# Weight sums of the paired tiles moved from VectorE to accumulating DMAs, and the first stage's splits in another order

## The chip, the cores and the metric

The kernel runs on one core of one Trainium2 chip. The metric is the device time of one execution on that core, in microseconds (us); a result is the median of several runs.

## What is computed

One layer of a streaming encoder trunk, for a prompt of 1024 rows and a sample of 32 rows that share the weights. One combined input projection feeds two branches: a conformer convolution module (GLU, causal depthwise convolution of width 31, layer norm, swish, a SiLU gate) and a Mamba-2 mixer (short convolution, SSD scan in chunks, gated RMS norm). Their outputs are gated, merged, projected, and added to the input and to a gated per-layer embedding.

```python
proj = x @ w_in + b_in                     # x: 1056 x 1024, all branch inputs and gates
u = a_val * sigmoid(a_glu)
u = causal_dwconv(u, ...)                  # width 31: the "taps"
u = silu(layer_norm(u)) * silu(a_gate)
xs, B, C = silu(causal_dwconv(xbc, ...))   # width 4
dt = softplus(dt_raw + dt_bias)
y, h = ssd_scan(xs, dt, A, B, C, h0)
out_b = gated_rmsnorm(y, z) @ w_b_out
merged = sigmoid(g_a) * (u @ w_a_out) + sigmoid(g_b) * out_b
out = layer_norm(alpha * x + merged @ w_out + sigmoid(g_p) * (p @ w_ple))
```

The part that the change touches is the first 48 weight tiles of `x @ w_in` (128 output columns each), the product `p @ w_ple`, and the softplus of `dt` that is worked out beside them.

## The kernel before

Everything is held transposed: 1056 columns (1024 + 32 rows of x, NT in the code) by 128 partitions. An fp32 product is made of three matmuls in the form fp32r (`three`): each operand is split into a rounded part "h" and the rest "l", and w_h x_l, w_l x_h and w_h x_h are summed in PSUM. ScalarE rounds (`act`, line 186), VectorE subtracts (`tt`, line 172: "l" = raw - "h"), so every split is one instruction on each of the two. `load` (line 189) issues from SyncE, in the order of the code, loads as well as stores; an issue waits there until its destination buffer is free and its source is ready, and what is behind it waits too. Matmuls are line 192 (`mm`). `stt` is line 176, `tsc` 181 and 183.

*The first stage* (lines 416 to 796) splits the columns of x (`x_split` for the blocks B11, B12, B21, B22 and the difference D1; `t_split` for the sums N2, T3, T4, which `x_sum` forms in place in the raw tiles `xraw`), makes the embedding product `p @ w_ple` and the dt product. `ple_group(m, g)` is one of 8 x 3 groups of six matmuls; ScalarE evicts each to a tile `pl`, and after the third of an m the tile is stored to the DRAM scratch `d_ple`. The tiles `pl` of m = 0 to 3 are units of a pool U (7 units, handed out in a ring and given back at the store), those of m = 4 to 7 lie in the buffers t3h and t3l. The weights of `p @ w_ple` are four tiles, wq0 to wq3, loaded by `wq_load` and split by `wq_split`. Between groups, `step(n)` takes the next n entries from a list `work` (splits, sums). After the first 12 groups come wq2 and wq3's splits, the 48 matmuls of the dt product (`dt_products`), N2's split, the split of the first pair weight, `dt1`, and then the last 12 groups.

*The pair slots*, s = 1 to 24, one for a pair i = s - 1 of weight tiles. A pair's weights are four 128 x 512 blocks r11, r12, r21, r22 (256 KB each), and the two output tiles are formed from seven products in place of eight, with weights

| product | 0 | 1 | 2 | 3 | 4 | 5 | 6 |
|---|---|---|---|---|---|---|---|
| weight | r11 | r21 + r22 | r11 + r21 + r22 | r12 | r11 + r21 | r12 + r11 + r21 + r22 | r22 |

and X-side operands B11, B12, N2, B21, T3, B22, T4. Each product is 24 matmuls. The tile "sx" carries weights 1, 2 and 5 in turn, and r21 is turned into weight 4 in place. In the profile the split weights are w_0h, w_0l to w_6h, w_6l, and the raw blocks are called r. After product j, `pair_slot` evicts what is finished (ScalarE writes a bank of PSUM out, VectorE adds or subtracts later ones), runs the stages of other work that are due (`run`), and then `prep_act(i, j)` and `prep_dve(i, j)`: a written-out order of the rounding, the subtractions, the sums and the loads by which pair i + 1 is made ready and pair i + 2 loaded. A sum must have its parts loaded, and a part can be loaded anew only when its last reader is done.

*What else runs in these slots.* `todo` holds stages (ld0, ld, st, d0, a0, d1 after product 0; a1 after 2; pm, a2 after 4; d2 after 5; pe, end) into which other work puts its steps: the gates (`ga`, `gb`, stored to `d_gate` by SyncE), `cbS` (ScalarE, from a gate tile, slot 6), the base tiles (`bt`, loaded from x and `d_ple`, stored to `d_base`), the GLU (`uin`, `sg`), the short convolution (`vin`, `cb`), and dt2 to dt10 in slots 1 to 5. dt2 (slot 1, after product 0) is the softplus on VectorE; dt3 (slot 1, after product 2) has two memsets on GpSimd, lines 647 and 648; dt4 (slot 1, after product 5) scans with what they wrote, line 658. Last, `run_fill(limit)` pulls the taps of the width-31 convolution (`cae`, `cao`) from a list until a running estimate of VectorE's time in the slot, `dve[0]`, reaches the limit. What the estimate leaves free is filled with taps as long as the list has any.

After slot 24 a slot is one weight tile, 8 k x 3 groups of 352 columns (`slot`; slots 25 to 67), and then the output projections follow.

Of the kernel before, what the change touches and what calls it, by code (L numbers as in the profile page):

```python
# [129 lines left out]
def emit(nc, tc, I, O, ctx):  # L130
# [57 lines left out]
    def load(dst, src):  # L188
        nc.sync.dma_start(dst, src)
# [305 lines left out]

    def pw_sum(i, dst, a, b):
        if i < len(PAIRS):
            if (i, dst) not in pr:
                pr[i, dst] = raw_tile(dst, f"{dst}_{i}")
            tt(pr[i, dst], pr[i, a], pr[i, b], ALU.add)  # L500
# [264 lines left out]
    for q in range(2):
        t_split("n2", (1, 1), q)
    pw_hi(0, 0, "r11")
    pw_lo(0, 0, "r11")
    dt1()
    pw_sum(0, "sx", "r21", "r22")  # L770
    pw_sum(0, "r21", "r11", "r21")
    pw_load(1, "r11")
    work.extend(xs4("D1") + [(pw_hi, 0, 1, "sx"), (pw_lo, 0, 1, "sx"), (pw_sum, 0, "sx", "r21", "r22"), (pw_hi, 0, 2, "sx"),
                             (pw_lo, 0, 2, "sx")] + xs2("T4"))
# [14 lines left out]
    pw_sum(0, "sx", "r12", "sx")
    pw_load(1, "r12")  # L790
    pw_hi(0, 4, "r21")
    pw_lo(0, 4, "r21")
# [993 lines left out]
```

## Time and profile before

| | |
|---|---|
| median of the runs | 1592.32 us (1592.23 to 1593.13, 3 runs) |
| the profiled execution | 1592.68 us, of which 1591.0 us are the span from its first to its last instruction |
| granted TensorE clock, mean | 0.984 |
| instructions | 26642 |
| the chain that ended last | PE 76%, DVE 12%, DMA 5%, ACT 4% |
| DMA | 208.43 MB, queues busy 41.9% of 16 engines' span; HBM read 156.49 MB, written 50.19 MB |

PE is TensorE, DVE VectorE, ACT ScalarE, POOL GpSimd, SP SyncE, and SPq SyncE's DMA queue. A row of a timeline is the start in us, the duration, the engine, the line, the operation, out<-in with tile names, shape and type, and in brackets how long the engine had idled before and what ended that. A row of waits is who waits, for what, then the total in us, the number of waits and the longest. Times count from the first instruction.

### The profile page before, as it was taken

The page shows a single profiled execution, that of the slowest core. Times are in us where ns is not written, and L with a number is a line of the kernel's source. Part 1 is how long each engine was busy: PE and PEld are TensorE (multiplying, and loading weights), DVE is VectorE, ACT ScalarE, POOL GpSimd, SP SyncE. Part 2 cuts the span into 40 slices and gives each one's busy share as a digit, 9 for nine tenths or more (in the row PEclk, how much of TensorE's full clock was granted, in tenths as well). Part 3 has the DMA queues.
Part 4 walks back from the last instruction along what each step waited for, and adds up shares of the span by engine and source line. Part 5 has one row for each costly group of instructions (what it writes and reads, how often), then busy time and mean ns, then how long its engine had stood idle before and what let it go on. Part 6 is the DMA issues. An engine that isn't in the chain of part 4 may idle for free.

```text
span 1591.0 us, 26642 instructions
## 1 busy us (share of the span) xinstructions
PE 1527.2 (96%) x10823; PEld 1481.8 (93%) x10823; DVE 1296.9 (82%) x1763; ACT 808.6 (51%) x1391; POOL 3.0 (0%) x14
## 2 busy tenths in 40 slices
PE   7899999999999989999999999999798999999997
PEld 6899999999999989999999999999688999999997
DVE  6888899999898599988988889888666887676654
ACT  6654334433434556666675666576564543333333
POOL 0000000000000000000000000000000000000000
PEclk9999999999999999999999999999899999999998
DMA  7252444442231134424252542336636171587422
GB/s 254 108 203 98 155 136 137 136 157 103 87 116 55 55 101 89 112 69 123 77 120 66 110 106 63 88 106 187 187 136 240 61 249 57 199 331 257 144 87 78
DMA packets 134377, 208.43 MB, mean 131 GB/s; under 512 B 28071, under 2 KB 84391, under 8 KB 134254
## 3 DMA queue, kind: packets, MB, share of 16 engines
q1 hardware_dynamic: 134254, 206.72, 41.9%
q8 instruction: 85, 1.39, 0.4%
q14 instruction: 38, 0.31, 0.1%
HBM read 156.49 MB, written 50.19 MB: 130 GB/s over the span
## 4 chain that ended last, share of the span: by engine, by line
PE 76%; DVE 12%; DMA 5%; ACT 4%; issue 2%; SPq 0%; DVEq 0%; ACTq 0%
PE ps L192 75%; DMA d_base<-cb_t 1%; PE ps L992 1%; DVE cao_u L176 1%; DVE cae_u L176 1%; DMA d_yn<-cbo_t 1%; DMA L_t<-d_accp 1%; DMA cat_t<-d_ca 1%; DVE sx L172 1%; DVE cb_t L176 0%; DVE wlo L172 0%; DMA d_gate<-ga_t 0%; DVE dt_u L176 0%; DVE acc_t L172 0%; DVE cb_u L176 0%
## 5 line engine op out<-in xcount | busy, mean ns | idle before, releaser
L176 DVE SCALAR_TENSOR_TENSOR cae_u<-uin_u,par,cae_u 128x1086 f32<-128x1086 f32 x120 | 161.3, 1344 | 0.0
L176 DVE SCALAR_TENSOR_TENSOR cao_u<-uin_u,par,cao_u 128x1086 f32<-128x1086 f32 x112 | 150.5, 1344 | 0.0
L186 ACT ACTIVATE whi<-wraw 128x1024 fp32r<-128x1024 f32 x65 | 68.5, 1054 | 67.5 <-PE ps L192 42.8
L186 ACT ACT_TABLE_LOAD x77 | 98.8, 1283 | 7.1 <-DMA out_conv_b<-vin_t 4.9
L172 DVE TENSOR_TENSOR wlo<-wraw,whi 128x1024 fp32r<-128x1024 f32 x65 | 79.3, 1219 | 24.6 <-ACT whi L186 24.5
L186 ACT ACTIVATE vin_t<-ps,par 128x352 f32<-128x352 f32 (+5 forms) x88 | 39.1, 476 | 107.3 <-PE ps L192 107.3
L186 ACT ACTIVATE L_t<-L_t,tk 128x128 f32<-128x128 f32 (+1 forms) x272 | 80.4, 381 | 0.0
L176 DVE SCALAR_TENSOR_TENSOR cb_t<-vin_t,par,cb_t 128x1059 f32<-128x1059 f32 x60 | 79.1, 1319 | 1.2
L186 ACT ACTIVATE zt_t<-ps,par 128x352 f32<-128x352 f32 x48 | 26.4, 554 | 75.3 <-PE ps L192 75.0
L172 DVE TENSOR_TENSOR acc_t<-acc_t,ps 128x352 f32<-128x352 f32 x72 | 36.6, 518 | 33.1 <-PE ps L192 33.0
L186 ACT ACTIVATE gb_t<-ps,par 128x528 f32<-128x528 f32 x26 | 18.2, 701 | 88.7 <-PE ps L192 74.8
L172 DVE TENSOR_TENSOR M<-ps,E 128x512 f32<-128x512 f32 (+1 forms) x32 | 20.4, 637 | 49.0 <-PE ps L192 45.3
L192 PE MATMUL ps<-n2l,w_2h 128*128 128x264 f32 x192 | 55.5, 289 | 3.7 <-ACT ga_t L186 3.7
L192 PE MATMUL ps<-t3l,w_4h 128*128 128x264 f32 x192 | 54.6, 284 | 2.3 <-ACT ga_t L186 2.3
L192 PE MATMUL ps<-n2h,w_2l 128*128 128x264 f32 x192 | 55.2, 288 | 0.0
L192 PE MATMUL ps<-n2h,w_2h 128*128 128x264 f32 x192 | 55.1, 287 | 0.0
L192 PE MATMUL ps<-t4l,w_6h 128*128 128x264 f32 x192 | 54.6, 285 | 0.3 <-ACT gb_t L186 0.3
L192 PE MATMUL ps<-t3h,w_4l 128*128 128x264 f32 x192 | 54.5, 284 | 0.0
L192 PE MATMUL ps<-t4h,w_6h 128*128 128x264 f32 x192 | 54.4, 284 | 0.0
L192 PE MATMUL ps<-t4h,w_6l 128*128 128x264 f32 x192 | 54.4, 283 | 0.0
L192 PE MATMUL ps<-t3h,w_4h 128*128 128x264 f32 x192 | 54.3, 283 | 0.0
L192 PE MATMUL ps<-x0l_t,whi 128*128 128x352 f32 x117 | 41.9, 358 | 8.9 <-ACT sg_t L186 5.0
(878 smaller groups left out, 5910.4 us busy)
## 6 DMA issues: line engine op xcount, KB each, us to landing
r<-in_w SPq DMA_DIRECT2D x96, 256.0 KB, 3.1
wraw<-in_w SPq DMA_DIRECT2D x39, 512.0 KB, 4.3
L_t<-d_accp SPq DMA_DIRECT2D x30, 512.0 KB, 6.5
d_yn<-cbo_t SPq DMA_DIRECT2D x16, 528.0 KB, 3.6
wraw<-in_wb SPq DMA_DIRECT2D x16, 512.0 KB, 3.6
yraw_t<-d_yn SPq DMA_DIRECT2D x15, 528.0 KB, 7.7
gs_t<-d_gate SPq DMA_DIRECT2D x15, 528.0 KB, 5.9
E<-d_expa SPq DMA_DIRECT2D x56, 128.0 KB, 4.7
```

Source lines behind the costliest of these rows:

```text
L172: nc.vector.tensor_tensor(out, a, b, op)
L176: nc.vector.scalar_tensor_tensor(out, a, s, b, op0, op1)
L186: nc.scalar.activation(out, a, f, **kw)
L192: nc.tensor.matmul(out, l, r, start=start, stop=stop, skip_group_check=more)
L992: nc.tensor.transpose(pX[:nt, j * P:(j + 1) * P], XS[j][:, sl], ident)
```

## The change

The sums of a pair's weights are no longer made by VectorE. Each summed weight gets a tile of its own, s1 (weight 1), s2 (weights 2 and then 5) and s3 (weight 4). SyncE loads the first part into it, and the further parts are added by DMAs that GpSimd issues with `accum_op=ALU.add`: s1 = 21 + 22, s2 = 11 + 21 + 22, to which `pw_s4` adds 12 after weight 2 has been split, and s3 = 21 + 11. So a pair has six loads from SyncE in place of four, and five accumulating DMAs from GpSimd, all of 256 KB; the four additions on VectorE go. r21 is no longer held by itself, and the buffers are r11, r12, r22, s1, s3 with one each and s2 with two. `prep_act` and `prep_dve` have another order: the loads of r11 and s2 for pair i + 2 and of r22 for pair i + 1 stand after product 1, s1 after 3, r12 after 5, s3 after 6, and weight 5 is rounded after product 0 of the following slot.

In the first stage, the splits of wq2 and wq3 come ahead of the sums T3 and N2, N2's and the first weight's splits come from the list `work`, `dt1` comes after D1's four splits in the list that runs beside the last 12 groups, and the tiles `pl` lie elsewhere: those of m = 0 and 1 in n2l, 2 and 3 in t3l, 4 and 5 in t3h, 7 in t3l, and only that of m = 6 is a unit of U. The raw weights of dt, w0, lie in the pair stage's buffer o0h in place of t3l.

```diff
-    RTAG = {"r11": 1, "r12": 1, "r21": 2, "r22": 2, "sx": 1}
+    RTAG = {"r11": 1, "r12": 1, "r22": 1, "s1": 1, "s2": 2, "s3": 1}
...
-    w0 = xpool.tile([P, 8, H], F32, tag="t3l", name="w0", bufs=1)
+    w0 = ppw.tile([P, 8, H], F32, tag="o0h", name="w0", bufs=1)
...
+    PARTS = {"r11": ("11",), "r12": ("12",), "r22": ("22",), "s1": ("21", "22"), "s3": ("21", "11"), "s2": ("11", "21", "22")}
...
     def pw_load(i, n):
         if i < len(PAIRS):
-            t = raw_tile(n, f"{n}_{i}")
-            load(t, I["w1"][2 * i + (n[1] == "2"), :, 512 * (n[2] == "2"):512 * (n[2] == "2") + 512])
-            pr[i, n] = t
+            t = pr[i, n] = raw_tile(n, f"{n}_{i}")
+            load(t, pw_src(i, PARTS[n][0]))
+            for q in PARTS[n][1:]:
+                nc.gpsimd.dma_start(t, pw_src(i, q), accum_op=ALU.add)
+
+    def pw_s4(i):
+
+        if i < len(PAIRS):
+            nc.gpsimd.dma_start(pr[i, "s2"], pw_src(i, "12"), accum_op=ALU.add)
...
     def prep_act(i, pos):
         if pos == 0:
+            pw_hi(i, 5, "s2")
             pw_hi(i, 6, "r22")
-        for j, n in {0: ((0, "r11"),), 2: ((1, "sx"),), 4: ((2, "sx"), (3, "r12")), 5: ((4, "r21"),), 6: ((5, "sx"),)}.get(pos, ()):
+        for j, n in {0: ((0, "r11"),), 2: ((1, "s1"),), 3: ((2, "s2"),), 4: ((3, "r12"),), 5: ((4, "s3"),)}.get(pos, ()):
             pw_hi(i + 1, j, n)
 
     def prep_dve(i, pos):
         if pos == 0:
-            pw_lo(i, 5, "sx")
-            pw_sum(i + 1, "sx", "r21", "r22")
+            pw_lo(i, 5, "s2")
         elif pos == 1:
             pw_lo(i, 6, "r22")
             pw_lo(i + 1, 0, "r11")
-            pw_sum(i + 1, "r21", "r11", "r21")
             pw_load(i + 2, "r11")
+            pw_load(i + 1, "r22")
+            pw_load(i + 2, "s2")
         elif pos == 3:
-            pw_lo(i + 1, 1, "sx")
-            pw_sum(i + 1, "sx", "r21", "r22")
+            pw_lo(i + 1, 1, "s1")
+            pw_load(i + 2, "s1")
+        elif pos == 4:
+            pw_lo(i + 1, 2, "s2")
+            pw_s4(i + 1)
         elif pos == 5:
-            pw_lo(i + 1, 2, "sx")
             pw_lo(i + 1, 3, "r12")
-            pw_sum(i + 1, "sx", "r12", "sx")
             pw_load(i + 2, "r12")
         elif pos == 6:
-            pw_lo(i + 1, 4, "r21")
-        if pos == 2:
-            pw_load(i + 2, "r21")
-            pw_load(i + 2, "r22")
+            pw_lo(i + 1, 4, "s3")
+            pw_load(i + 2, "s3")
...
-        if g == 0 and m in (4, 6):
-            both = xpool.tile([P, 2, NT], F32, tag=f"t3{'hl'[m // 2 - 2]}", name=f"pl{m}", bufs=1)
+        if g == 0 and m in (0, 2, 4, 7):
+            both = xpool.tile([P, 2, NT], F32, tag={0: "n2l", 2: "t3l", 4: "t3h", 7: "t3l"}[m], name=f"pl{m}", bufs=1)
...
-    work.extend(xs4("B11") + xs4("B12") + xs2("D1") + [(wdt_split,)] + xs4("B21") + xs4("B22") + xs2("T3") + xs2("N2"))
+    work.extend(xs4("B11") + xs4("B12") + xs2("D1") + [(wdt_split,)] + xs4("B21") + xs4("B22") + [(wq_split, 2), (wq_split, 3)])
...
-    for i in (2, 3):
-        wq_split(i)
+    pw_load(0, "r22")
+    work.extend(xs2("T3") + xs2("N2") + ts2("n2", (1, 1)) + [(pw_hi, 0, 0, "r11"), (pw_lo, 0, 0, "r11")])
+    step(len(work))
     for k in range(8):
         dt_products(k)
...
-    dt1()
...
+    work.extend(xs4("D1") + [(dt1,), (pw_load, 1, "r11"), (pw_hi, 0, 1, "s1"), (pw_lo, 0, 1, "s1"), (pw_load, 1, "s1"), (pw_hi, 0, 2, "s2"),
+                             (pw_lo, 0, 2, "s2"), (pw_s4, 0), (pw_load, 1, "s2")] + xs2("T4"))
```

On ScalarE in the first stage, the rows around the tenth eviction of `pl` (it fills the tile of m = 3 from bank ps13) stand before as follows; wq2h and wq3h are the rounding of the third and fourth w_ple tile, n2h that of N2, x7h the last of the splits of x.

```order
L186 ACTIVATE x6h_t13_116<-xraw_u4_152 128x528
L186 ACTIVATE pl_u8_309<-ps13_302 128x352
L186 ACTIVATE x7h_t15_118<-xraw_u4_152 128x528
L186 ACTIVATE pl_u8_309<-ps14_314 128x352
L186 ACTIVATE pl_u8_309<-ps15_324 128x352
L186 ACTIVATE wq2h_334<-wq2_155 128x512
L186 ACTIVATE wq3h_338<-wq3_157 128x512
L186 ACTIVATE n2h_3_4_390<-xraw_u3_150 128x1056
L186 ACTIVATE n2h_3_4_390<-xraw_u4_152 128x1056
L186 ACTIVATE w0_0h_396<-r11_0_162 128x512
L186 ACT_TABLE_LOAD
```

And now the same stretch, where pl2 is the tile of m = 2 and 3 in t3l, and pl4 that of m = 4 and 5.

```order
L186 ACTIVATE x6h_t13_116<-xraw_u4_152 128x528
L186 ACTIVATE pl2_276<-ps13_307 128x352
L186 ACTIVATE x7h_t15_118<-xraw_u4_152 128x528
L186 ACTIVATE wq2h_317<-wq2_155 128x512
L186 ACTIVATE pl2_276<-ps14_321 128x352
L186 ACTIVATE wq3h_329<-wq3_157 128x512
L186 ACTIVATE pl2_276<-ps15_333 128x352
L186 ACTIVATE n2h_3_4_348<-xraw_u3_150 128x1056
L186 ACTIVATE n2h_3_4_348<-xraw_u4_152 128x1056
L186 ACTIVATE w0_0h_354<-r11_0_162 128x512
L186 ACTIVATE pl4_413<-ps16_406 128x352
```

The unit u8 of the ring U no longer takes the eviction, the two w_ple splits have moved ahead of the last two evictions, and behind w0_0h comes the first eviction of the last 12 groups, where the table load of `dt1` stood.

On GpSimd, from the memset of the dt weights (the last instruction of its set-up) on, before:

```order
L212 MEMSET mask_76 128x128
L213 AFFINE_SELECT mask_76<-mask_76 128x128
L465 MEMSET wdt_143 128x8x64
L647 MEMSET dt3_u12_403 32x1056
L648 MEMSET dt3_u12_403 32x17
```

And now, where the number behind s1, s2, s3 is the pair, line 489 is the accumulating DMA of `pw_load`, 494 that of `pw_s4`, and 651 and 652 are the memsets of dt3:

```order
L464 MEMSET wdt_143 128x8x64
L489 DMA s1_0_164<-in_w1 128x512
L489 DMA s2_0_167<-in_w1 128x512 x2
L489 DMA s3_0_173<-in_w1 128x512
L489 DMA s1_1_518<-in_w1 128x512
L494 DMA s2_0_167<-in_w1 128x512
L489 DMA s2_1_552<-in_w1 128x512 x2
L489 DMA s3_1_574<-in_w1 128x512
L489 DMA s2_2_672<-in_w1 128x512 x2
L651 MEMSET dt3_u8_459 32x1056
L652 MEMSET dt3_u8_459 32x17
L489 DMA s1_2_743<-in_w1 128x512
```

The memsets that the scan of dt4 reads now stand on GpSimd behind the two accumulating DMAs into s2 of pair 2.

On SyncE in slot 6 (before with pair 6's r12, then two loads of x for the base tiles and two stores of gates):

```order
L189 DMA r12_6_1804<-in_w1 128x512
L189 DMA bt_u21_1865<-in_xT 128x1056
L189 DMA bt_u22_1867<-in_xT 128x1056
L189 DMA d_gate_94<-ga_t37_1596 128x1056
L189 DMA d_gate_94<-gb_t38_1597 128x1056
```

And now:

```order
L189 DMA r12_6_1833<-in_w1 128x512
L189 DMA s3_6_1863<-in_w1 128x512
L189 DMA bt_u18_1895<-in_xT 128x1056
L189 DMA bt_u19_1897<-in_xT 128x1056
L189 DMA d_gate_94<-ga_t37_1620 128x1056
L189 DMA d_gate_94<-gb_t38_1621 128x1056
```

The load of s3 stands between r12 and the four transfers of the base and gate tiles.

More of the change, by code (lines that the diff above doesn't have):

```diff
@@ L417, in emit @@
     wq = []
-    QTAG = ("r12", "sx", "r21", "r21")
-    RTAG = {"r11": 1, "r12": 1, "r21": 2, "r22": 2, "sx": 1}
+    RTAG = {"r11": 1, "r12": 1, "r22": 1, "s1": 1, "s2": 2, "s3": 1}
     def raw_tile(tag, name):
@@ L427, in wq_load @@
     def wq_load(i):
-        wq.append([raw_tile(("r12", "sx", "r21", "r22")[i], f"wq{i}")])
+        wq.append([raw_tile(("r12", "s1", "r22", "s2")[i], f"wq{i}")])
         load(wq[i][0], I["wp"][i])
@@ L478, in emit, with pw_src @@
     pr, pw = {}, {}
+    PARTS = {"r11": ("11",), "r12": ("12",), "r22": ("22",), "s1": ("21", "22"), "s3": ("21", "11"), "s2": ("11", "21", "22")}
+    def pw_src(i, q):
+        return I["w1"][2 * i + (q[0] == "2"), :, 512 * (q[1] == "2"):512 * (q[1] == "2") + 512]
     def pw_load(i, n):
         if i < len(PAIRS):
-            t = raw_tile(n, f"{n}_{i}")
-            load(t, I["w1"][2 * i + (n[1] == "2"), :, 512 * (n[2] == "2"):512 * (n[2] == "2") + 512])
-            pr[i, n] = t
+            t = pr[i, n] = raw_tile(n, f"{n}_{i}")
[5 more added lines that the diff above has]
+            nc.gpsimd.dma_start(pr[i, "s2"], pw_src(i, "12"), accum_op=ALU.add)
     def pw_hi(i, j, n):
@@ L494, in pw_lo @@
             tt(l_, pr[i, n], h_[:, :].bitcast(F32), ALU.subtract)
[L496 to L500, printed above, removed]
     def prep_act(i, pos):
         if pos == 0:
+            pw_hi(i, 5, "s2")
             pw_hi(i, 6, "r22")
-        for j, n in {0: ((0, "r11"),), 2: ((1, "sx"),), 4: ((2, "sx"), (3, "r12")), 5: ((4, "r21"),), 6: ((5, "sx"),)}.get(pos, ()):
+        for j, n in {0: ((0, "r11"),), 2: ((1, "s1"),), 3: ((2, "s2"),), 4: ((3, "r12"),), 5: ((4, "s3"),)}.get(pos, ()):
             pw_hi(i + 1, j, n)
@@ L575, in ple_group @@
             three(ps[:, :GN], wh[:, w], wl[:, w], ph[:, k, c0:c1], pl_[:, k, c0:c1], k == 0, k == 1)
-        if g == 0 and m in (4, 6):
-            both = xpool.tile([P, 2, NT], F32, tag=f"t3{'hl'[m // 2 - 2]}", name=f"pl{m}", bufs=1)
+        if g == 0 and m in (0, 2, 4, 7):
+            both = xpool.tile([P, 2, NT], F32, tag={0: "n2l", 2: "t3l", 4: "t3h", 7: "t3l"}[m], name=f"pl{m}", bufs=1)
             pls[m], pls[m + 1] = both[:, 0, :], both[:, 1, :]
-        if g == 0 and m < 4:
+        if g == 0 and m == 6:
             pls[m] = U.get([P, NT], F32, "pl")
@@ L583, in ple_group @@
             load(d_ple[m], pls[m])
-            if m < 4:
+            if m == 6:
                 U.put(pls[m])
@@ L743, in step @@
             f(*a)
-    for n in ("r11", "r21", "r22", "r12"):
+    for n in ("r11", "s1", "s2", "r12", "s3"):
         pw_load(0, n)
@@ L753, in emit @@
     xs2 = lambda n: [(x_sum, n, q) for q in range(2)]
-    work.extend(xs4("B11") + xs4("B12") + xs2("D1") + [(wdt_split,)] + xs4("B21") + xs4("B22") + xs2("T3") + xs2("N2"))
+    ts2 = lambda n, q: [(t_split, n, q, i) for i in range(2)]
+    work.extend(xs4("B11") + xs4("B12") + xs2("D1") + [(wdt_split,)] + xs4("B21") + xs4("B22") + [(wq_split, 2), (wq_split, 3)])
     for m in range(4):
@@ L760, in emit @@
     step(len(work))
-    for i in (2, 3):
-        wq_split(i)
+    pw_load(0, "r22")
+    work.extend(xs2("T3") + xs2("N2") + ts2("n2", (1, 1)) + [(pw_hi, 0, 0, "r11"), (pw_lo, 0, 0, "r11")])
+    step(len(work))
     for k in range(8):
         dt_products(k)
[L765 to L768, printed above, removed]
-    dt1()
[L770 to L774, printed above, removed]
+    work.extend(xs4("D1") + [(dt1,), (pw_load, 1, "r11"), (pw_hi, 0, 1, "s1"), (pw_lo, 0, 1, "s1"), (pw_load, 1, "s1"), (pw_hi, 0, 2, "s2"),
+                             (pw_lo, 0, 2, "s2"), (pw_s4, 0), (pw_load, 1, "s2")] + xs2("T4"))
     for m in range(4, 8):
@@ L781, in emit @@
     x_put((1, 1))
-    for n in ("r21", "r22"):
-        pw_load(1, n)
     pw_hi(0, 3, "r12")
     pw_lo(0, 3, "r12")
+    pw_load(1, "r12")
     for q in range(2):
@@ L788, in emit @@
     x_put((0, 1))
[L789 to L792, printed above, removed]
+    pw_hi(0, 4, "s3")
+    pw_lo(0, 4, "s3")
+    pw_load(1, "s3")
     for q in range(2):
@@ L795, in emit @@
     x_put((1, 0))
-    pw_hi(0, 5, "sx")
     new_psum("ps1")
@@ L1465, in half_load @@
     def half_load(q):
-        pr["h", q] = raw_tile(("r11", "r21")[q], f"half{q}")
+        pr["h", q] = raw_tile(("r11", "s1")[q], f"half{q}")
         load(pr["h", q], I["w_src"][S_CL][:, 512 * q:512 * q + 512])
```

## Prediction

> **What bounds the kernel now.** First the page's busy times and windows by stage, then TensorE's waits stage by stage, then the engines' timelines where it waits. From the page and one table of windows (columns: window, length, then busy time and count of PE, PEld, DVE, ACT, POOL; granted clock, DMA share, GB/s):
>
> ```profile
> PE 1527.2 (96%) x10823; PEld 1481.8 (93%) x10823; DVE 1296.9 (82%) x1763; ACT 808.6 (51%) x1391; POOL 3.0 (0%) x14
> ...
> 20.00:40.00 20.00, 14.24 (x73) 13.43 (x72) 14.96 (x25) 9.93 (x19) 0.00 (x0) 0.83 0.48 184
> 60.00:80.00 20.00, 18.67 (x140) 18.24 (x138) 18.91 (x31) 9.05 (x17) 1.09 (x2) 0.92 0.15 53
> 160.00:200.00 40.00, 37.33 (x305) 36.91 (x305) 34.93 (x43) 14.89 (x23) 0.00 (x0) 1.00 0.49 161
> 200.00:520.00 320.00, 320.00 (x2636) 320.00 (x2635) 291.30 (x368) 128.28 (x216) 0.00 (x0) 1.00 0.34 114
> ```
>
> TensorE is the bound: 1527 of 1591 us. From 200 to 520 us, most of the pair slots, it never pauses, although VectorE is 91% busy beside it. There a matmul takes 320/2636 = 0.121 us, a product of 24 takes 2.91 us, a slot of seven 20.4 us. Work taken off VectorE in that stretch buys nothing by itself; the change can only win where TensorE waits. Its waits, from three windows (0 to 80, 80 to 200, 500 to 620) and one late (1060 to 1240; columns: total us, times, longest):
>
> ```profile
> PE ps L192 <- DVE wq2l L172: 4.4, 1, 4.4
> PE ps L192 <- ACT ga_t L186: 3.7, 1, 3.7
> ...
> PE ps L192 <- DVE ga_t L172: 2.3, 3, 1.5
> PE ps L192 <- ACT ga_t L186: 2.3, 1, 2.3
> PE ps L192 <- DVE sg_t L172: 1.3, 1, 1.3
> ...
> PE ps L192 <- ACT sg_t L186: 5.0, 1, 5.0
> PE ps L192 <- DVE vin_t L172: 3.5, 1, 3.5
> ...
> PE ps L192 <- ACT acc_t L186: 6.9, 4, 4.4
> PE ps L192 <- DVE M L172: 6.9, 1, 6.9
> ```
>
> The late ones lie beyond slot 57; by the order, the list of conv taps is as long in both kernels from slot 49 on, so I leave them at zero. What can move is about 8 us in the prologue, 6 us in slots 2 to 7, 8.5 us around slots 24 and 25.
>
> **The change, part by part.** The sums that go (columns: count, total us, mean ns, idle before), and the two loads between which an accumulating DMA must lie (size, us to landing):
>
> ```profile
> L172 DVE TENSOR_TENSOR sx<-r,r 128x512 f32<-128x512 f32 x48 | 33.2, 692 | 1.7
> L172 DVE TENSOR_TENSOR r<-r,r 128x512 f32<-128x512 f32 x24 | 16.4, 684 | 0.0
> L172 DVE TENSOR_TENSOR sx<-r,sx 128x512 f32<-128x512 f32 x24 | 16.4, 684 | 0.0
> ...
> r<-in_w SPq DMA_DIRECT2D x66, 256.0 KB, 3.1
> wraw<-in_w SPq DMA_DIRECT2D x39, 512.0 KB, 4.3
> ```
>
> VectorE loses 33.2 + 16.4 + 16.4 = 66 us, 2.7 us a slot. Where conv taps are in stock, the order fills the space with them at once; only in slots without taps (1 to 4, 8, 9, 13, 17, 18) does it get ahead.
>
> No accumulating DMA is in this trace. It fetches 256 KB and also reads 256 KB at its destination, so I bound it by 3.1 us (a plain load of its size) and 7.5 us (between the 7.0 of the wait for a d_gate store and the 8.0 of a d_ple store, below), and take 3.7, the middle of the two rows above. GpSimd's own share of an issue is unseen too: 0 to 1.1 us, I take 0.7, above an SP issue. The Trainium skill ("DMA: Bandwidth & Descriptors", section "Anatomy of one DMA — SWDGE (gpsimd) path") gives about 2.0 us and the bytes over 436 GB/s, by which I estimate 2.6 us here; plain loads of that size took 3.1, above that rule, so the rows stand.
>
> *Prologue.* ScalarE, its issuer's stores, VectorE, GpSimd and two TensorE starts:
>
> ```profile
> 27.75 0.46 ACT L186 ACTIVATE pl_u<-ps 128x352 f32<-128x352 f32 x1 [5.97 <-PE ps L192]
> 28.11 0.63 ACT L186 ACTIVATE x7h_t<-xraw_u 128x528 fp32r<-128x528 f32 x1
> ...
> 33.02 2.25 ACT L186 ACTIVATE n2h<-xraw_u 128x1056 fp32r<-128x1056 f32 x2 [2.53 <-DVE xraw_u L176]
> ...
> 48.59 1.51 ACT L186 ACTIVATE pl<-ps 128x352 f32<-128x352 f32 x4
> ...
> 20.50 9.29 SPq L189 DMA_DIRECT2D d_ple<-pl_u  x4
> ...
> d_ple<-pl_u SPq DMA_DIRECT2D x4, 528.0 KB, 8.0
> ...
> 54.74 1.26 DVE L172 TENSOR_TENSOR t3l<-xraw_t,t3h 128x1056 fp32r<-128x1056 f32 x1 [2.40 <-DMA d_ple<-pl]
> ...
> 60.63 0.29 DVE L183 TENSOR_SCALAR dt_u<-dt_u 128x264 f32<-128x264 f32 x1
> ...
> 68.61 0.69 DVE L172 TENSOR_TENSOR w_5l<-sx,w_5h 128x512 fp32r<-128x512 f32 x1
> ...
> 77.49 2.35 DVE L658 TENSOR_TENSOR_SCAN dtc_t<-dt_u,dt_u 32x1056 f32<-32x1056 f32 x1
> 79.77 0.67 DVE L172 TENSOR_TENSOR ga_t<-ga_t,ps 128x528 f32<-128x528 f32 x1
> ...
> 68.80 0.97 POOL L647 MEMSET dt_u<- 32x1056 f32 x1 [66.14 <-DVE dt_u L176]
> ...
> 59.08 0.39 PE L192 MATMUL ps<-n2l,w_2h 128*128 128x264 f32 x1 [3.69 <-ACT ga_t L186]
> ...
> 80.49 0.39 PE L192 MATMUL ps<-x0l_t,w_1h 128*128 128x264 f32 x1 [1.49 <-DVE ga_t L172]
> ```
>
> The tenth `pl` eviction takes a U unit still being stored: 20.5 + 8.0 is about the 27.75 at which it ran, although the view names PE. In the new code `pl` lies in other buffers, so x7h follows at about 22, and the `w_ple` splits stand ahead of the T3 and N2 sums: the 4.4 us wait goes, n2h starts near 29.1 in place of 33.0 (the splits and four sums now fill VectorE from 22.8), and the last `pl` eviction ends near 44.7 in place of 50.1, 5.4 us earlier. t3l waits for the store behind it, so it, dt2 and w_5l come 5.3 us earlier: dt2 at 55.3, w_5l at 63.3. ScalarE no longer has w_5h ahead of the ga_t eviction, so product 2 of slot 1 starts near 51.4 in place of 59.08.
>
> Then two waits are next. Product 5 would start at 51.4 + 3 x 2.91 = 60.1 but needs w_5l, which stands behind dt2: 63.9. And GpSimd's memset for the scan, done 7 us early today, now stands behind the accumulates for pair 2, whose buffer w_5l frees: w_5l, w_6l, w_0l to 65.1; two SP issues ahead of the load 0.9 (the two bt loads below took 0.91); load 3.1, landing at 69.1; first accumulate 3.7, second's issue 0.7, memsets 1.1: 74.6; scan 2.35, ga_t 0.6: slot 2's product 1 starts at 77.6. Queued behind the scan are that ga_t, w_4l and slot 2's dt work; TensorE alone is hurt, being ready at 63.9 + 8.7 = 72.6. Against 80.49 it gains 2.9. But the 3.69 us wait at 59.08 left the clock at 0.92 of 20 us, some 1.6 us lost, while the 2.3 us wait for ACT ga_t, which lies in the window from 160 to 200, left that window at 1.00; a 3 to 5 us pause here will cost about half that: 0.8. Net gain **2.1**, from 4 (everything lands in 3.1) to a loss of 3 (7.5). The Trainium skill ("TensorE: Matmul & The Clock Gate", "Part 1: The HAM clock gate") has the clock halve after an idle window of about 3.4 us; the 2.3 and 3.69 waits agree, and by it the pause at slot 2 would cost the full 1.6.
>
> *Slots 2 to 4.* The waits at the starts of slots 3 and 4 (0.4 of the 2.3 for DVE ga_t, 1.3 for sg_t) come from VectorE running late in slots without taps; 2.7 us less a slot hides both: gain **1.7**. What is late next there is the fourth accumulate for w_5h, with the whole slot as cover.
>
> *Slot 6.* Here ScalarE waits for a store, and TensorE (2.3) for ScalarE:
>
> ```profile
> 164.85 0.91 SPq L189 DMA_DIRECT2D bt_u<-in_xT  x2
> 165.85 0.38 SPq L189 DMA_DIRECT2D d_gate<-ga_t  x1
> ...
> 164.94 0.69 DVE L172 TENSOR_TENSOR w_4l<-r,w_4h 128x512 fp32r<-128x512 f32 x1
> ...
> 173.21 1.08 ACT L186 ACTIVATE cbS_t<-ga_t 128x1056 f32<-128x1056 f32 x1 [7.02 <-DMA d_gate<-ga_t]
> ```
>
> SP's last load of a slot, s3, now waits for w_4l (done near 165.6) and stands ahead of bt and d_gate: 1.25 us later. Beside their 2.1 MB come one load and one accumulate, 0.5 to 0.75 MB at 7 us for 2.1: 1.7 to 2.5 us if all lies on the path. I take **2.5 lost** in all, bounds -2.3 (the lighter prologue separates them) and +4. Behind cbS on ScalarE stand w_6h, w_0h and the evictions.
>
> *Slots 23 to 25.* The order puts a tap ahead of the add that ends slot 23 in place of two moved steps, so the 3.5 stays. In slot 24 this tap, ahead of the short conv, goes, which takes 1.3 off the 5.0: gain **1.3**, bounds 0 and 2.5.
>
> ```profile
> 556.54 1.35 DVE L176 SCALAR_TENSOR_TENSOR cao_u<-uin_u,par,cao_u 128x1086 f32<-128x1086 f32 x1
> ```
>
> *Steady slots.* Traffic rises by seven 256 KB transfers a slot: 1.84 MB/20.4 us = 90 GB/s on 114, share 0.34 to about 0.61, and 0.8 with the accumulates' second reads. Cost zero, under the cover of the loop worked out as a rival below.
>
> *Sum:* 2.1 + 1.7 - 2.5 + 1.3 = 2.6 us off the profiled execution's 1592.68 (span 1591.0 and 1.7 outside it), so 1590.1. The median of the runs, 1592.32, lies 0.4 below that execution: **1589.7**.
>
> **The rivals.** *GpSimd's loop becomes the bound (slower).* Each slot, s2 for pair i+2 can load only after w_5l, and w_5l of the next slot needs the accumulate that waits in the same in-order queue behind s2's two and s1's one. Two rows of slot 7:
>
> ```profile
> 190.53 0.68 DVE L172 TENSOR_TENSOR w_5l<-sx,w_5h 128x512 fp32r<-128x512 f32 x1
> ...
> 193.72 0.68 DVE L172 TENSOR_TENSOR w_0l<-r,w_0h 128x512 fp32r<-128x512 f32 x1
> ```
>
> From w_5l's end to w_0l's 3.2, SP 1.0, load 3.1, two accumulates to landing 2L, two issues 1.4, w_5h and w_5l 1.3: 10.0 + 2L against 20.4. It decides from L = 5.2 us. At 3.7 there are 3 us to spare; at 6.2 it is 2 us a slot in the twelve slots full of taps (5 to 7, 10 to 12, 14 to 16, 19 to 21): 24 us, 1614. For it: 528 KB transfers took 7 to 8 us when the queues were full; against: the share of 0.34.
>
> *The prologue pays in full.* If ScalarE's earlier start isn't eaten at the memset and the gate's store lands in time, slot 2 gains 4, slot 6 gains 2.3 and the rest 3: 1592.3 - 9.3 + some 2 for the w_5l wait = 1585. For it, light traffic before 80 us (share 0.15); against, the memset's place in the order.
>
> *The waits for DMA spread.* Slot 6's pattern recurs at slots 8, 11 and 13; with 2 to 3 us more at each and at slot 2, 1592.3 - 3 + 4 x 2.5 = 1599.
>
> **How the numbers follow.** Some 0.2%, 3.2 us, is what a measurement of this kernel can tell from no change, so "faster" is below 1589.1. The sum, with its terms' bounds, holds 0.50: 1586.5 to 1592.5, of which 0.22 lies below that line and 0.28 above it. The prologue in full: 0.20. GpSimd's loop: 0.22. Spread waits: 0.08. So faster 0.42, same 0.28, slower 0.30. The likeliest case's own range is 1586.5 to 1592.5; the range for 8 in 10 goes from 1584 to 1606, which leaves out the dearer half of the loop's cases.
>
> **What would show it.** Right: slot 2's product 1 starts at 76 to 79 us, and the scan ahead of it waits for POOL; x7h at 22; cbS waits 8 to 11 us; no PE wait in 200 to 520; an accumulate lands in 3.5 to 5 us. Wrong: w_5h waiting for its DMA slot after slot with PE pauses between 200 and 520 (the loop), or slot 2 starting before 75.

## The result, and the profile after

The changed kernel takes 1674.79 us (median of 4 runs, 1669.75 to 1677.06) against 1592.28 us before: a ratio of 1.0513, 95% interval 1.0489 to 1.0538. It is 82 us slower. The profiled execution took 1674.84 us, with a span of 1673.1 and a granted clock of 0.968.

From the page, the busy times (VectorE has lost 61 us, GpSimd has 105 more), and from the table of windows the pair stage:

```profile
PE 1552.7 (93%) x10823; PEld 1503.3 (90%) x10823; DVE 1236.3 (74%) x1667; ACT 805.4 (48%) x1391; POOL 107.6 (6%) x134
```

```profile
80.00:200.00 120.00, 103.28 (x779) 102.22 (x780) 78.66 (x100) 45.93 (x87) 18.25 (x21) 0.92 0.73 196
200.00:520.00 320.00, 279.64 (x2165) 276.06 (x2164) 208.84 (x245) 103.63 (x174) 56.57 (x65) 0.95 0.68 179
```

TensorE, which had no gap from 200 to 520 us, now stands for 40 of these 320 us, and issues 2165 matmuls there in place of 2636, at a granted clock of 0.95 in place of 1.00. The starts of the pair slots (the first x0l_t, w_0h matmul of each) say the same: slot 1 starts at 45.97 us in place of 49.39, slot 24 at 619.60 in place of 533.07. A slot takes 573.6/23 = 24.9 us in place of 21.0, and 90 us are lost on the way, less the 3.4 of the earlier start; some 4 come back behind slot 24. Who waits for a DMA there is in ScalarE's waits (total us, times, longest), and how long these DMAs take is at the foot of the view of one line (494, the addition of r12):

```profile
ACT w_5h L186 <- DMA s<-in_w: 123.1, 21, 11.0
```

```profile
DMA to landing us min/median/max: 4.9/7.3/11.6
```

In 21 of 24 slots the rounding of weight 5 waits for the last addition into its tile. The chain that ended last shows one round of it (start, length, what; "issue" is time for which the profile names nothing that was waited for, here the first addition on its way):

```profile
266.55 0.64 ACT w_5h L186
...
267.21 0.06 DVE w_5l L172
...
268.42 0.69 DVE w_0l L172
...
269.51 0.43 SPq L189
...
270.04 4.09 DMA s<-in_w
...
274.80 0.86 POOL s L489
275.65 3.12 issue
...
278.81 0.60 POOL s L489
...
279.56 0.54 POOL s L489
280.10 10.19 DMA s<-in_w
...
290.31 0.03 ACT w_5h L186
```

From w_5h to the next w_5h 23.8 us pass, and no step of it is TensorE's: VectorE frees the tile s2, SyncE loads its first part (4.1), GpSimd adds the second (0.86 to issue, 3.1 to landing), issues the third, then the addition for s1, and only then that of r12, which lands 10.2 us later. The list of DMA issues for the windows 274 to 276 and 278.7 to 281.5 (count, size, median us to landing) shows how much an addition's place matters:

```profile
s<-in_w POOLq DMA_DIRECT2D x1, 256.0 KB, 3.6
...
s<-in_w POOLq DMA_DIRECT2D x3, 256.0 KB, 9.4
...
bt_u<-d_ple SPq DMA_DIRECT2D x1, 528.0 KB, 9.0
```

One addition alone on the queue landed in 3.6 us; of three issued within 2 us the median took 9.4. Two loads of 528 KB for the base tiles fell into that second window too, so these rows alone don't part the place in the queue from the traffic beside it. The experiments do.

### The profile page after: what moved, and what is told of

It reads as the page before. It is cut to its first block, busy times and chain, and to the rows that moved or that the text cites. A ratio compares the mean times of both kernels' runs of the same rounds, so it can differ in the third digit from the quotient of the medians.

```text
span 1673.1 us, 26947 instructions
## 1 busy us (share of the span) xinstructions
PE 1552.7 (93%) x10823; PEld 1503.3 (90%) x10823; DVE 1236.3 (74%) x1667; ACT 805.4 (48%) x1391; POOL 107.6 (6%) x134
## 3 DMA queue, kind: packets, MB, share of 16 engines
q0 software_dynamic: 17280, 31.46, 11.3%
## 4 chain that ended last, share of the span: by engine, by line
PE 59%; DVE 13%; DMA 13%; issue 7%; ACT 5%; POOL 1%; SPq 1%; DVEq 0%; POOLq 0%; ACTq 0%
PE ps L192 58%; DMA s<-in_w 7%; DVE cae_u L176 2%; POOL s L489 1%; DVE cao_u L176 1%; DMA d_base<-cb_t 1%; SPq L189 1%; DMA d_yn<-cbo_t 1%; PE ps L987 1%; DMA bt_t<-in_xT 1%; DMA L_t<-d_accp 1%; DMA cat_t<-d_ca 1%; DMA d_gate<-ga_t 1%; DVE cb_t L176 0%; DMA bt_u<-in_xT 0%
## 5 line engine op out<-in xcount | busy, mean ns | idle before, releaser
L489 POOL DMA_DIRECT2D s<-in_w x96 | 83.2, 922 | 497.3 <-DMA s<-in_w 309.1
L172 DVE TENSOR_TENSOR wlo<-wraw,whi 128x1024 fp32r<-128x1024 f32 x65 | 79.2, 1219 | 22.2 <-ACT whi L186 22.2
L192 PE MATMUL ps<-t3l,w_4h 128*128 128x264 f32 x192 | 60.2, 314 | 29.8 <-ACT ga_t L186 18.5
L172 DVE TENSOR_TENSOR w_5l<-s,w_5h 128x512 fp32r<-128x512 f32 x24 | 16.5, 689 | 85.4 <-ACT w_5h L186 85.4
L186 ACT ACTIVATE w_5h<-s 128x512 fp32r<-128x512 f32 x24 | 15.1, 629 | 123.1 <-DMA s<-in_w 123.1
L192 PEld LDWEIGHTS ps<-t3l,w_4h 128*128 128x128 f32 x192 | 40.3, 210 | 32.3 <-ACT ga_t L186 20.1
L192 PE MATMUL ps<-t3h,w_4l 128*128 128x264 f32 x192 | 58.5, 305 | 0.0
L192 PE MATMUL ps<-t3h,w_4h 128*128 128x264 f32 x192 | 58.2, 303 | 0.0
```

The lines of the kernel that those rows point to most:

```text
L172: nc.vector.tensor_tensor(out, a, b, op)
L186: nc.scalar.activation(out, a, f, **kw)
L192: nc.tensor.matmul(out, l, r, start=start, stop=stop, skip_group_check=more)
L489: nc.gpsimd.dma_start(t, pw_src(i, q), accum_op=ALU.add)
```

## Experiments

Theory 1: GpSimd's in-order queue makes a loop over w_5l, the load of s2 two pairs ahead, its additions and r12's. Theory 2: the traffic slows every transfer. Theory 3: an addition is slow by itself. Ratios are against the kernel before on the same chip, with their 95% interval; us are worked out from them at 1592.3.

**e1: r12's addition first.** Only GpSimd's order changes: r12's addition goes ahead of those into s2 and s1 of the pair behind, which are issued later for it.

```diff
         elif pos == 4:
             pw_lo(i + 1, 2, "s2")
             pw_s4(i + 1)
+            pw_add(i + 2, "s2")
+            pw_add(i + 2, "s1")
```

(and the loads of s2 and s1 at 1 and 3 no longer issue their additions.)

> Same instructions as the changed kernel; only GpSimd's order differs: the addition of r12 to s2 of pair i+1 (which weight 5 waits for) is issued before the additions into s2 and s1 of pair i+2, not behind them. Theory 1 (the in-order queue of GpSimd makes a loop: w_5l, load of s2 two pairs ahead, its two additions, then the addition of r12, w_5h, w_5l): the loop is cut, the wait of ScalarE's w_5h for its DMA (123 us in all) falls below 20 us, slots go back to 20.4 us, and the time to 1588 to 1597, 1591 likeliest (before, less the 3.4 us by which the pair stage now starts earlier, plus some for base and gate transfers). Theory 2 (the added traffic slows every transfer, the order matters little): the time stays above 1650. Theory 3 (an addition in DMA is slow by itself): as theory 1, since its landing is then off the path, but with additions that still take 5 to 6 us.

1633.38 us, ratio 1.0261 (1.0241 to 1.0282): 41.6 us over before, so half of the loss is the order of the same instructions on one queue. ScalarE's waits, then r12's addition:

```profile
ACT w_1h L186 <- DMA s<-in_w: 66.7, 14, 8.6
...
ACT w_5h L186 <- DMA s<-in_w: 6.9, 4, 3.7
```

```profile
DMA to landing us min/median/max: 3.8/4.0/9.8
```

The loop over w_5h is gone (123.1 to 6.9 us), and r12's addition now lands in 4.0 us in place of 7.3. But the time I had expected, 1591, was missed by 42: w_1h waits in w_5h's place, since s1's addition now stands behind both of s2 (e8 moves it), and slots 3, 4 and 6 still take 27.1, 30.0 and 31.0 us.

**e2: the new first stage alone**, with the sums on VectorE as before.

```diff
-    work.extend(xs4("B11") + xs4("B12") + xs2("D1") + [(wdt_split,)] + xs4("B21") + xs4("B22") + xs2("T3") + xs2("N2"))
+    work.extend(xs4("B11") + xs4("B12") + xs2("D1") + [(wdt_split,)] + xs4("B21") + xs4("B22") + [(wq_split, 2), (wq_split, 3)])
...
+    work.extend(xs4("D1") + [(dt1,), (pw_sum, 0, "sx", "r21", "r22"), (pw_sum, 0, "r21", "r11", "r21"), (pw_load, 1, "r11"),
```

> The kernel before with the first stage of the changed kernel and the sums on VectorE: the tiles pl in n2l, t3l and t3h, the w_ple splits ahead of T3 and N2, dt1 later. The sums, loads and their order in the pair slots are those of before. The pair stage started 3.4 us earlier in the changed kernel. All theories: 1589 to 1592, 1590 likeliest, since dt2 and the scan of slot 1 stand ahead of what slots 1 and 2 wait for; 1592.3 or more if the whole lead is lost at those two places.

1588.39 us, ratio 0.9978 (0.9967 to 0.9988): 3.5 us faster, good to some 2, and a little more than I had expected. Slot 1 starts at 45.44, slot 24 at 528.44 in place of 533.07. This is the one half of the change that pays, and this kernel beats both.

**e3: the additions alone**, with the first stage of before.

```diff
-        if g == 0 and m in (0, 2, 4, 7):
-            both = xpool.tile([P, 2, NT], F32, tag={0: "n2l", 2: "t3l", 4: "t3h", 7: "t3l"}[m], name=f"pl{m}", bufs=1)
+        if g == 0 and m in (4, 6):
+            both = xpool.tile([P, 2, NT], F32, tag=f"t3{'hl'[m // 2 - 2]}", name=f"pl{m}", bufs=1)
...
+    dt1()
+    pw_load(1, "r11")
+    work.extend(xs4("D1") + [(pw_hi, 0, 1, "s1"), (pw_lo, 0, 1, "s1"), (pw_load, 1, "s1"), (pw_hi, 0, 2, "s2"),
```

> The changed kernel with the first stage of before (old pl tiles, old order of splits, dt1 early); the sums are still made by accumulating DMAs. Theory 1: the loop alone makes the loss, so 1674.8 plus the 3.4 us of the first stage, 1675 to 1681. If the new first stage is itself part of the loss (its later dt1 and the memset behind the additions start the slots late), 1655 to 1670.

1684.37 us, ratio 1.0584 (1.0555 to 1.0612): 93 us. The loss is wholly that of the new way to make the sums (additions, six loads and their order), none of it the first stage's. The new first stage seems worth more beside it (11 us, good to some 6) than alone; I had expected 3.4.

**e4: the additions as plain writes.**

```diff
-                nc.gpsimd.dma_start(t, pw_src(i, q), accum_op=ALU.add)
+                nc.gpsimd.dma_start(t, pw_src(i, q))
```

> The changed kernel with every accumulating DMA made a plain one that overwrites its destination: the same 120 transfers from GpSimd in the same order with the same waits, no addition, so the weights of products 1, 2, 4 and 5 are single blocks and the sums are left out. Theory 1 (order and issue on GpSimd): 1655 to 1675, the landing stays near 5 us. Theory 3 (the addition makes the transfer slow): landing near 3.1 us as a plain load from SyncE, the loop is then some 18 us, below the slot, and the time at most 1610. Theory 2 (traffic): a third of the added bytes read goes, 1620 to 1650.

1637.76 us, ratio 1.0289 (1.0263 to 1.0314), between the ends of theories 1 and 3. All of GpSimd's transfers (the last number is the median landing) and its queue (packets, MB, share of 16 engines' span), first in the changed kernel, then in this one:

```profile
s<-in_w POOLq DMA_DIRECT2D x120, 256.0 KB, 5.5
...
q0 software_dynamic: 17280, 31.46, 11.3%
```

```profile
s<-in_w POOLq DMA_DIRECT2D x120, 256.0 KB, 3.7
...
q0 software_dynamic: 9600, 31.46, 6.1%
```

So adding costs 1.8 us of a landing in this crowd, and nearly twice the packets and engine time for the same 31.46 MB. The Trainium skill ("DMA: Bandwidth & Descriptors", section "Rules for kernel authors") says that an accumulating DMA reads its destination and writes it later; the longer landings and the added packets agree, though the read has no row of its own. By the medians, with the prediction's 10.0 us for the rest, the loop is now 10.0 + 3.4 (the additions of line 489) + 4.7 (r12's) = 18.1 us, under a slot. Yet 46 us are lost, and w_5h still waits in 15 slots, 42.7 us in place of 123.1. So there is likely a second cause, which e5 looks for. r12's write, then the wait for it:

```profile
DMA to landing us min/median/max: 3.4/4.7/7.6
```

```profile
ACT w_5h L186 <- DMA s<-in_w: 42.7, 15, 10.6
```

**e5: no DMA from GpSimd at all.**

```diff
-            for q in PARTS[n][1:]:
-                nc.gpsimd.dma_start(t, pw_src(i, q), accum_op=ALU.add)
```

> The changed kernel without any of GpSimd's DMAs: each summed weight is its first part alone (the sums are left out); SyncE's six loads a pair and their order are those of the changed kernel. With the additions re-ordered 41 us were left, in slots 3, 4, 6 (27 to 31 us) and at 8 and 11 to 14. Theory A (what is left is SyncE's order: its load of s3 waits for w_4l and holds up the slot's other transfers, among them W_out's and the base tiles'): slots 3, 4 and 6 stay above 23 us, and the time is 1598 to 1612. Theory B (what is left is the additions' traffic and GpSimd's queue): all slots at 20.4 to 23 us and the time 1584 to 1591, that of the first stage alone.

(`pw_s4` issues nothing either.) 1607.72 us, ratio 1.0103 (1.0082 to 1.0123): 16 us lost without one addition, slots 4 and 6 at 28.6 and 30.0. That is what theory A forecast, but for slot 3, which takes 22.2 us and not more than 23; e9 puts the theory to the test. SyncE and VectorE at the start of slot 3, which begins at 91.27 (wsum is VectorE's reduction of W_out's tiles):

```profile
94.04 0.33 SPq L189 DMA_DIRECT2D s<-in_w  x1
94.41 0.43 SPq L189 DMA_DIRECT2D uin_u<-in_cache_a  x1
95.28 0.33 SPq L189 DMA_DIRECT2D cw_t<-in_wo  x1
```

```profile
93.32 0.69 DVE L172 TENSOR_TENSOR w_4l<-s,w_4h 128x512 fp32r<-128x512 f32 x1
...
98.62 1.22 DVE L1142 TENSOR_REDUCE wsum<-cw_t 128x8 f32<-128x1024 f32 x1 [4.58 <-DMA cw_t<-in_wo]
```

The load of s3 waits for w_4l, the last of VectorE's splits, and W_out's tiles (cw) stand behind it on SyncE, 4.0 us into the slot. VectorE waits 4.58 us for them and with it everything behind, slot 4's splits and transfers too.

**e6: additions of 64 columns**, in the changed kernel's order.

```diff
-                nc.gpsimd.dma_start(t, pw_src(i, q), accum_op=ALU.add)
+                nc.gpsimd.dma_start(t[:, :64], pw_src(i, q)[:, :64], accum_op=ALU.add)
```

> The changed kernel with each addition cut to 64 of the 512 columns (32 KB in place of 256; the sums of the other columns are left out): the same 120 issues, waits and order on GpSimd, an eighth of the bytes. Bytes decide an addition's time: landing 2 to 3 us, the loop of GpSimd below the slot, time within 10 us of the kernel with no additions. A fixed price per addition decides (issue 0.85 us and a latency): landing stays above 4 us and the time above 1640.

1623.97 us, ratio 1.0203 (1.0174 to 1.0231): 32 us, 16 more than with none, between the two forecasts. An eighth of the bytes still lands in 2.8 us, and w_5h still waits 23.6 us (9 times), so in this order both bytes and a fixed price count:

```profile
s<-in_w POOLq DMA_DIRECT2D x120, 32.0 KB, 2.8
```

**e7: s3 loaded late**, on top of e1.

```diff
         if pos == 0:
             pw_lo(i, 5, "s2")
+            pw_load(i + 1, "s3")
...
             pw_lo(i + 1, 4, "s3")
-            pw_load(i + 2, "s3")
```

> The kernel with r12's addition first, and SyncE's load of s3 taken from the end of a slot, where it waits for w_4l ahead of the next slot's transfers, to the place behind them (after product 0). All sums as in the changed kernel. Theory A (SyncE's order): slots 3, 4 and 6 lose 4 to 8 us each, and the time falls from 1633 to 1608 to 1620, the loop over w_1h staying. Theory B (traffic and GpSimd's queue): no change within 5 us.

1610.04 us, ratio 1.0115 (1.0096 to 1.0134): 23 us less than e1. (s3's addition moves with its load, so GpSimd's order changes a little too.) Slot 3 is back at 20.4 and slot 6 at 25.0; slot 4 stays at 28.3, where I had expected 4 to 8 us off, because VectorE waits there for a W_out tile that was issued in time and landed late, beside GpSimd's additions:

```profile
106.31 11.16 DMA cw_u<-in_wo
```

w_1h still waits for its addition:

```profile
ACT w_1h L186 <- DMA s<-in_w: 58.4, 15, 8.5
```

**e8: the additions spread**, on top of e7.

```diff
+            pw_add(i + 2, "s2", slice(1, 2))
         elif pos == 4:
...
-            pw_add(i + 2, "s2")
             pw_add(i + 2, "s1")
+            pw_add(i + 2, "s2", slice(2, 3))
```

> As the kernel with s3 loaded late, and GpSimd's additions of a slot are spread: s3 after product 0, the first of s2 after product 3, then r12 to s2, s1, and the second of s2 last; s1 no longer stands behind both additions of s2. If the order on GpSimd's queue is what makes w_1h wait (66.7 us after the first re-ordering), these waits fall below 15 us and the time to 1592 to 1605; if five additions of 6 us each are too many for a slot of 20.4 us in any order (31 us when one waits for the next), another weight waits in w_1h's place and the time stays above 1615.

1612.17 us, ratio 1.0123 (1.0098 to 1.0148): the same as e7, and between the two forecasts. The waits for w_1h's DMA are gone from the list, w_4h (21.1 us), w_5h (17.5) and w_2h (6.2) wait instead, 45 us in all where e7 had 87 (w_1h, w_4h and w_5h). What that saves is lost in slots 4 and 6, which take 31.5 and 29.0 us (28.3 and 25.0 in e7). This re-ordering of five additions a slot gained nothing.

**e9: no additions, s3 late.** e5 with e7's move:

```diff
         if pos == 0:
             pw_lo(i, 5, "s2")
+            pw_load(i + 1, "s3")
...
-            pw_load(i + 2, "s3")
```

> The kernel without GpSimd's DMAs (the sums are left out), with SyncE's load of s3 taken from behind w_4l to the place after product 0. That kernel with s3 in its old place took 1607.7, 19 us over the new first stage alone (1588.4). Theory A (SyncE's order makes those 19 us: s3's load holds up W_out's and the base tiles' transfers): slots 4 and 6 fall from 28.6 and 30.0 us to 21 to 23.5 and the time to 1586 to 1592. Theory B (six loads in place of four, or VectorE's other order, make them): at least 1600.

1593.45 us, ratio 1.0004 (0.9993 to 1.0015; this chip ran the kernel before at 1593.45). The move takes off 16 of e5's 16.4 us; slots 4 and 6 take 22.1 and 24.1 (slot 6 and the time lie just above theory A's ranges, and the time under theory B's 1600). So s3's load behind w_4l is what e5 had lost. SyncE now issues the same tile 2.7 us before slot 3 (at 92.19), and VectorE doesn't wait:

```profile
89.54 0.43 SPq L189 DMA_DIRECT2D cw_t<-in_wo  x1
```

```profile
94.88 1.19 DVE L1141 TENSOR_REDUCE wsum<-cw_t 128x8 f32<-128x1024 f32 x1
```

Against e2 some 4 us stay. Slots 2 to 4 take 62.9 us in place of e2's 66.0, so VectorE's lighter load, with its other order, does gain 3.1 us there; but slots 11 and 20 are 2.8 and 4.5 us longer than 20.4, and slot 6 is 1.3 longer than in e2. In slot 11 (VectorE, then TensorE) taps and base tiles fill the time that the sums left, ahead of the add that frees a PSUM bank. That is read from the rows and wasn't tried by itself:

```profile
264.65 1.34 DVE L176 SCALAR_TENSOR_TENSOR cae_u<-uin_u,par,cae_u 128x1086 f32<-128x1086 f32 x1
265.91 0.70 DVE L172 TENSOR_TENSOR ga_t<-ga_t,ps 128x528 f32<-128x528 f32 x1
```

```profile
266.66 0.39 PE L192 MATMUL ps<-x0l_t,w_1h 128*128 128x264 f32 x1 [2.55 <-DVE ga_t L172]
```

**e10: s3 late alone**, the same move in the changed kernel, with its additions:

```diff
         if pos == 0:
             pw_lo(i, 5, "s2")
+            pw_load(i + 1, "s3")
...
-            pw_load(i + 2, "s3")
```

> The changed kernel with this one move alone: SyncE's load of s3 (and its addition on GpSimd) from the end of a slot to after product 0 of the next. GpSimd's order stays: r12's addition behind those of s2 two pairs ahead. If the two orders cost each for itself, 1674.8 less the 23 us that the move gave after r12's addition had gone first: 1645 to 1657. If GpSimd's loop sets the slots anyway and SyncE's order is hidden under it: 1665 to 1675.

1680.88 us, ratio 1.0565 (1.0533 to 1.0597), against 1.0513 (1.0489 to 1.0538) for the changed kernel. The two intervals touch, so it isn't clear that the move costs anything; it gains nothing while the loop sets the slot. The time is a little above both forecasts. Slots 2 to 4 take 80.8 us, as in the changed kernel (81.3). In the profiled execution, which at 1692.24 us was the slowest of four, r12's addition lands in 8.1 us (median; 7.3 in the changed kernel) and w_5h waits longer:

```profile
ACT w_5h L186 <- DMA s<-in_w: 149.6, 22, 12.2
```

**e11: both orders mended, additions of 64 columns.** e7 with e6's cut:

```diff
-                nc.gpsimd.dma_start(pr[i, n], pw_src(i, q), accum_op=ALU.add)
+                nc.gpsimd.dma_start(pr[i, n][:, :64], pw_src(i, q)[:, :64], accum_op=ALU.add)
```

> The kernel with r12's addition first and s3 late (1610.0), each addition of the pair slots cut to 64 of 512 columns (the sums of the other columns are left out), so both orders are mended and the bytes are an eighth. If the bytes of the additions make what is left (21.6 us over the first stage alone: W_out's tiles landing in 11 us at slot 4, w_1h waiting 58 us), 1587 to 1593. If the issue and latency of each addition make it, 1600 to 1610.

1592.36 us, ratio 1.0002 (0.9990 to 1.0014), as without additions (e9). With the orders right, 120 issues and an eighth of the bytes cost nothing that shows in the medians, and what e7 had left is the additions' bytes: 1.0115 less 1.0002, 18 us. r12's addition of 32 KB, and the wait for w_1h that was 58.4 us in e7:

```profile
DMA to landing us min/median/max: 2.3/2.4/9.1
```

```profile
ACT w_1h L186 <- DMA s<-in_w: 7.5, 3, 3.0
```

Slot 4 doesn't follow this: in the profiled execution (1596.65 us, 4 over the median) it takes 26.1 us, where e7 has 28.3 and e9 22.1, and W_out's tile in the same place takes 9.69. So that late tile of e7 isn't mainly the additions' bytes; what makes it late stays open.

**e12: two additions a pair, the other two sums on VectorE.**

```diff
         elif pos == 3:
             pw_lo(i + 1, 1, "s1")
+            pw_sum(i + 1, "r11")
             pw_load(i + 2, "r11")
         elif pos == 5:
             pw_lo(i + 1, 2, "s1")
             pw_lo(i + 1, 3, "r12")
+            pw_sum(i + 1, "r12")
```

> All sums made, two of five by DMA: s1 = 21 + 22 and s3 = 21 + 11 by one addition each, weights 2 and 5 by VectorE (s1 + r11, then + r12), with s1 in two buffers, s3 loaded late, no addition in a row behind another in the same tile. Two transfers of 6 us a slot of 20.4 us, 1.4 us a slot less on VectorE than before. Theory (an addition costs nothing where its landing has half a slot of slack and SyncE's order is kept): 1587 to 1592, about the first stage alone (1588.4). If the added traffic costs in proportion (21.6 us for five): 1595 to 1599.

1595.16 us, ratio 1.0019 (1.0007 to 1.0031): 3.0 us over before, 6.5 over the first stage alone, and so neither free nor in proportion by e11's price (2/5 of 18 are 7, and with e9's 0.6 that would be 8 over before). Of the kernels that make all their sums and make some by DMA it is the fastest, but it is slower than e2, so VectorE's lighter load doesn't pay for it.

The steps, in us at 1592.3 (each between two ratios whose intervals are 0.1 to 0.25% to either side, so good to some 2 to 5 us). They hold in this order only: the same steps taken otherwise have other prices. Cutting the bytes in the changed kernel's order takes off 49 us (e6), s3's move gains nothing in that order (e10) and 16 us without additions (e5 to e9).

| from, to | what differs | us |
|---|---|---|
| before, e2 | first stage | -3.5 |
| e2, e9 | six loads, other order, refilled taps | +4.1 |
| e9, e11 | 120 additions of 32 KB from GpSimd | -0.3 |
| e11, e7 | the other 7/8 of the additions' bytes | +18.0 |
| e7, e1 | s3's load behind w_4l on SyncE (its addition with it) | +23.2 |
| e1, changed | r12's addition behind s2's and s1's on GpSimd | +40.1 |

## Why the prediction was wrong, point by point

**The step that failed** is in "GpSimd's loop becomes the bound": "two accumulates to landing 2L", with L = 3.7 for both. The path of the loop was right, and its sign of being wrong is what came: w_5h waits for its DMA in 21 of 24 slots, with TensorE's pauses between 200 and 520 us. The 10.0 us around the landings came out nearly right too (23.8 less the two landings, 3.1 and 10.2, is 10.5), but partly by luck: from w_5l's end to w_0l's 1.8 us pass in that round where I had 3.2, SyncE's load takes 4.1 in place of 3.1, and GpSimd's two gaps with its issues 2.9 in place of 1.4. 3.7 us is about what an addition takes alone (3.6 in the changed kernel, 3.7 median for r12's in e7). But r12's is the last of three in a row on one queue: 7.3 in the median, up to 11.6, and 4.0 when e1 puts it first. With 4.9, the median of the other additions, 10.0 + 4.9 + 7.3 = 22.2 us lies above a slot, and 2L = 7.4 hid it: the likeliest case should have been this rival, which had a chance of 0.22 and a price of 24 us. Its price was also too low, 2 us in twelve slots, where e1 takes off 40.

**"Cost zero" in the steady slots** failed for a second reason: 18 us are the additions' bytes (e7 to e11), which I had put at nothing under the cover of the loop, though the share worked out there was 0.61, and 0.8 with the second reads (it measured 0.68 from 200 to 520 us). The largest wait that goes with them is ScalarE's for w_1h, 58.4 us in e7 and 7.5 in e11.

**Slot 6** had the right place, and too small a size. Its row after:

```profile
191.62 1.08 ACT L186 ACTIVATE cbS_t<-ga_t 128x1056 f32<-128x1056 f32 x1 [11.68 <-DMA d_gate<-ga_t]
```

I had 8 to 11 us, it is 11.68, and slot 6 takes 30.4 us in place of 23.0. The mechanism, s3's load ahead of the gate's store, is there without additions: moving it cuts this wait from 11.0 us (e5) to 7.7 (e9). In the changed kernel it isn't the whole of it, since the wait is 11.71 in e10 as well: there the store is issued ahead of s3's load, but cbS runs 10.6 us later (at 189.95, after 179.36), in the changed kernel 8.5.

What I missed is that s3's load stands ahead of every slot's other transfers, W_out's above all (e5's rows). For slots 2 to 4 I had counted a gain of 1.7; they take 81.3 us in place of 66.0. The gain itself is real, 3.1 us in e9, but the first stage's pause (below), GpSimd's loop and s3's place cover it: e1 takes 77.5 there, e7 69.1, e10 80.8.

**The first stage** was right nearly to the row as far as slot 1. ScalarE, VectorE, GpSimd, TensorE:

```profile
22.30 0.70 ACT L186 ACTIVATE x7h_t<-xraw_u 128x528 fp32r<-128x528 f32 x1
```

```profile
55.40 0.29 DVE L183 TENSOR_SCALAR dt_u<-dt_u 128x264 f32<-128x264 f32 x1
...
63.51 0.68 DVE L172 TENSOR_TENSOR w_5l<-s,w_5h 128x512 fp32r<-128x512 f32 x1
...
77.29 2.35 DVE L662 TENSOR_TENSOR_SCAN dtc_t<-dt_u,dt_u 32x1056 f32<-32x1056 f32 x1 [6.33 <-POOL dt_u L652]
```

```profile
70.60 0.86 POOL L489 DMA_DIRECT2D s<-in_w  x1 [10.61 <-DVE w_3l L172]
75.26 0.84 POOL L489 DMA_DIRECT2D s<-in_w  x1 [3.80 <-DMA s<-in_w]
75.79 1.30 POOL L651 MEMSET dt_u<- 32x1056 f32 x1
```

```profile
64.25 0.39 PE L192 MATMUL ps<-x4h_t,w_5l 128*128 128x264 f32 x1 [2.31 <-DVE w_5l L172]
...
80.29 0.59 PE L192 MATMUL ps<-x0l_t,w_1h 128*128 128x264 f32 x1 [5.61 <-DVE ga_t L172]
```

x7h at 22, dt2 at 55.3, w_5l at 63.3 and product 5 at 63.9 were forecast. The scan does wait for GpSimd's memset behind the two additions. Only their size was off, 0.86 and 3.80 us for the first where I had 3.7, from a start at 70.6 in place of 69.1, so slot 2's product 1 starts at 80.29 and not at 77.6: of the 2.9 us gained there 0.2 are left.

The clock's price behind that pause was also too small. I had 0.8 us; from 80 to 100 us the granted clock is 0.85, where it was 1.00 before, and 141 matmuls are issued in place of 160, some 3.0 us of 20. Slot 3 starts at 100.43 in place of 98.09, so with the additions the stage brings a loss of 2 to 3 us where I had a net gain of 2.1 (bounds -3 to 4). Without additions on GpSimd it brings 3.5 us (e2), but there the memset waits for nothing, so that isn't a hit of the 2.1.

By the Trainium skill's sum for a DMA from GpSimd, 2.0 us and the bytes over 436 GB/s ("DMA: Bandwidth & Descriptors", section "Anatomy of one DMA — SWDGE (gpsimd) path"), the estimate for 256 KB is 2.6 us. Every addition of that size measured lies above it: 3.5 is the least (e7 and e8).

**Slot 25** came as forecast (1.3), the wait of 5.0 being 3.7 now. The other wait of this stretch, which was to stay at 3.5, is 4.4, so 0.4 of the 1.3 are left:

```profile
PE ps L192 <- DVE vin_t L172: 4.4, 1, 4.4
PE ps L192 <- ACT sg_t L186: 3.7, 1, 3.7
```
